# Paired activation halves in split fp32 products, with transposed modulation sums and a turned router product

## The chip, the cores and the metric

The kernel runs on one core of a Trainium2 chip. TensorE (PE) does the matrix products, VectorE (DVE), ScalarE (ACT) and GpSimd (POOL) the element-wise work, and sixteen DMA engines move data between HBM and SBUF. The metric is device time of one execution in microseconds (us); lower is better. Three runs of the kernel before took 2549.2, 2550.33 and 2555.16 us.

## The reference, cut to what matters

Everything is fp32. A first network of two layers works on 256 latent tokens and 256 context tokens of width 1024; a second block works on the 256 latent tokens alone. The parts that the change touches:

```python
# first network, layer l; cond is silu(c) for the latents, silu(c_ctx) for the context
m = cond @ w_ada[l] + b_ada[l]                       # (1024) @ (1024, 6144): the modulation
sh1, sc1, gt1, sh2, sc2, gt2 = split(m, 6)
xn = rms_norm(h, g_norm_mix[l]) * (1 + sc1) + sh1    # 512 tokens in all
p  = xn @ w_in[l]                                    # q, k, v, gates, ... of three branches
h  = h + gt1 * (sum_i sigmoid(gate_i) * (y_i @ w_branch[l, i])) @ w_out[l]
x2 = rms_norm(h, g_norm_ffn[l]) * (1 + sc2) + sh2
logits = x2 @ w_group, x2 @ w_router                 # 4 + 32 columns: the router
h  = h + gt2 * moe(x2)                               # top 2 of 32 experts
# in layer 1 the context gives only k and v, so queries and gates are 256 tokens
# second block, 256 tokens
z = rmsnorm(x, pre_mix_g) @ w_in_2                   # scan, short convolution, dilated attention
x = x + rmsnorm((sum_i sigmoid(h @ w_gate_i + b_i) * (y_i @ w_branch_2[i])) @ w_mix_out_2, post_mix_g)
gt = causal_dwconv(h @ w_ff_gate, ff_conv_w) + ff_conv_b
x = x + rmsnorm((gelu(gt) * (h @ w_ff_up)) @ w_ff_down, post_ffn_g)      # width 2816
```

## The kernel before, in words

**Split products.** PE's fast format (fp32r) drops low bits. So each factor of a dense product is split into a high part and a low rest, and three products are summed in one PSUM accumulator: high by high, high by low, low by high. A weight piece of 128 x 1024 values is copied by ACT to the high part `wh` (line 148), and DVE subtracts that from the raw weights to give `wl` (line 149). Each piece is split just before its use, with three buffers of `wh` and `wl` (four in the FFN), so DVE's and ACT's pace can hold PE.

**Two forms of dense product.** `dense_x` keeps activations stationary and streams 512 weight columns (lines 222 to 224); tokens end on partitions. `dense_w` keeps weights stationary and streams the tokens (lines 240 to 242); features end on partitions. The change is in `dense_w`: for one block of 128 output features (a column, below) and each 128 of the input it issues three products over n tokens. In layer 0 n is 512; in layer 1 and block 2 it is 256, and a product streams 256 columns. When a column's last product is done, its evacuation reads the accumulator: a gate's tanh on ACT, `G * acc` on DVE (line 454), in the FFN a scaled copy on ACT and two convolution steps on DVE (line 1623). Four accumulators of one PSUM bank each (512 fp32 values a partition) rotate.

**Modulation.** For the 24 pieces of 512 outputs (12 a layer) `ada_tile` multiplies with groups of array columns, which leaves partial sums on four groups of partitions; ACT copies them to `part`, and a product with the selection matrix `sel` adds them up. For the first eight pieces (shift and scale of the mixing) four small products give columns; for the other sixteen a single product of 512 columns in two passes gives a row (line 372). DVE adds a bias row that SP's queue has loaded, and POOL's queue writes the row to HBM scratch, from where it is read back broadcast. These pieces run as background between the products of the first layer's mixing; the queue of PE is in program order, and the order of instructions on each engine is set by the scheduler of the framework.

**Router.** For 256 tokens and each half of the features, `xr` (normalised tokens, features on partitions) is stationary and 36 columns of router weights stream: 16 passes (line 837). DVE scales the sums by the inverse root of the token's mean square.

The stretches, in us of the span: layer 0's mixing to some 640, its experts to 1130, layer 1's mixing 1240 to 1500, its experts to 1990, block 2's mixing to 2350 (scan, short convolution and gates 2036 to 2102, dilated attention to 2224, two more gated branches to 2317), FFN with gate and up 2352 to 2483, its last product to the end.

Of the kernel before, what the change touches and what calls it, by code (L numbers as in the profile page):

```python
# [8 lines left out]
FT = mybir.dt.float32  # L9
# [79 lines left out]

class Builder:  # L90
# [44 lines left out]
    def T(self, out, in_):  # L135
        k = in_.shape[0]
        self.nc.tensor.transpose(out, in_, self.ident[:k, :k])  # L137
# [55 lines left out]
    def dense_x(self, src, J, W, xh, xl, tts, evac, hold=0):  # L193

        if self.begun:
            ps, pieces, piece = self.begun.pop()
        else:
            self.tick()
            ps, pieces, piece = self.begin_x(src, J, W, xh, xl)
# [12 lines left out]
    def begin_x(self, src, J, W, xh, xl):  # L212
# [128 lines left out]
    def ada_tile(self, l, n, raw=None):  # L341
# [14 lines left out]
        if q < 2:  # L356
            for b in range(4):
                m = mm(ps[:, 2 * b:2 * b + 2], lhsT=part[:, b * 128:(b + 1) * 128], rhs=self.sel,
                       start=True, stop=True)
            if l == 0 and n in (0, 2):  # L360
                self.keep_warm(m, 6 if n else 3)
            for w in range(2):
                bias = self.vA[:, l * 48 + n * 4:l * 48 + n * 4 + 4]
                nc.vector.tensor_tensor(self.ada[l][:, q * 2 + w, half * 4:half * 4 + 4], ps[:, w:8:2], bias,
                                        op=OP.add)
            if q == 1:
                for w in range(2):
                    a = self.ada[l][:, 2 + w, half * 4:half * 4 + 4]
                    g = self.vA[:, 96 + l * 8 + half * 4:96 + l * 8 + half * 4 + 4]
                    nc.vector.scalar_tensor_tensor(a, a, 1.0, g, op0=OP.add, op1=OP.mult)  # L370
        else:
# [6 lines left out]
            if q == 4:  # L378
                gt = self.p_part.tile([2, 512], FT, name="grow", tag="row", bufs=2)
                nc.sync.dma_start(gt, bcast(I["g_norm_ffn"][l, half * 512:(half + 1) * 512], 2))  # L380
                nc.vector.scalar_tensor_tensor(row, row, 1.0, gt, op0=OP.add, op1=OP.mult)
            nc.gpsimd.dma_start(self.d_rows[l, q - 2, :, half * 512:(half + 1) * 512], row)
# [13 lines left out]
    def mix_norm(self, tp, l, h, mid=None, junk=None):  # L396

        nc = self.nc
        xh = self.p_x.tile([128, 8, 512], FR, name="xh", tag="xh")
        xl = self.p_x.tile([128, 8, 512], FR, name="xl", tag="xl")  # L400
# [11 lines left out]
        for k, (w, j) in enumerate(order):  # L412
            ws = slice(w * 256, w * 256 + 256)
            if k == 4 and mid is not None:
                mid(xh, xl)
# [8 lines left out]
            nc.vector.tensor_copy(xh[:, j:j + 2, ws], x)  # L424
            nc.vector.tensor_tensor(xl[:, j:j + 2, ws], x, xh[:, j:j + 2, ws].bitcast(FT), op=OP.subtract)
        return xh, xl

    def to_yT(self, y, n):

        yh = self.p_y.tile([128, 4, n], FR, name="yh", tag="yh")  # L430
        yl = self.p_y.tile([128, 4, n], FR, name="yl", tag="yl")
        for c in range(4):
# [3 lines left out]
            self.hilo(yh[:, c, :n], yl[:, c, :n], ps[:, :n])  # L436
        return yh, yl

    def gate_branch(self, i, gate_src, br_src, xh, xl, yh, yl, n, merged, bias=None):
        nc = self.nc  # L440
        for half in range(2):
# [15 lines left out]
            self.dense_w(gate_src[:, half * 512:(half + 1) * 512], 8, 512, xh, xl, n, ev_gate)  # L457
            self.dense_w(br_src[:, half * 512:(half + 1) * 512], 4, 512, yh, yl, n, ev_br)
# [31 lines left out]
    def mix(self, l, xh, xl):  # L490
# [19 lines left out]
        with self.tp("sg", 1, side="right") as sg:  # L510
# [15 lines left out]
            self.dense_x(W(O_ZB), 8, 512, xh, xl, tts, lambda t, ps: gelu2(u2[:, t], ps), hold=2)  # L526
# [14 lines left out]
            self.dense_x(W(O_ZB + 512), 8, 512, xh, xl, tts, ev_v)  # L541
            self.dense_x(W(O_VA), 8, 512, xh, xl, allt, lambda t, ps: nc.scalar.activation(v[:, t], ps, AF.Copy))
# [1268 lines left out]
```

## Time and profile before

| | |
|---|---|
| runs (us) | 2549.2, 2550.33, 2555.16; median 2550.33 |
| profiled execution | 2552.59 us, span 2550.6 us |
| granted TensorE clock | 0.983 mean |
| PE busy | 2431.7 us, 95% |
| DVE, ACT, POOL busy | 1334.0 us (52%), 857.1 us (34%), 134.6 us (5%) |
| DMA | 652.48 MB, 256 GB/s mean |

The profile is one execution. The profiled execution is 2.0 us longer than its span, and 2.3 us longer than the median. Busy shares are averages over stages with different limits, so a stretch is read by itself: a PE that is full there beside engines with room is the bound; where the DMA share is near 1, the transfers are. An engine's mean duration is a little longer than its pace, as successive instructions of one engine overlap; the pace is the distance of two starts in the timeline.

### The profile page before, as it was taken

To read this page: it belongs to the slowest core of one execution; us is meant where nothing else is said; L and a number is where in the kernel's file an instruction comes from. 1 tells how busy PE (TensorE), PEld (TensorE's weight loads), DVE (VectorE), ACT (ScalarE), POOL (GpSimd) and SP (SyncE) were. 2 spreads that over 40 slices of the span, in tenths; PEclk is the share of its full clock that TensorE was granted. 3 is DMA by queue.
4 is the path that set the end of the run, shared out by engine and by line. 5 is a ranking of instruction groups with operands and counts; after the bars stand their busy time and mean duration, and the time that the engine had idled before them with its cause. 6 is when DMAs were issued, how large, how long until landed. Compare 5 with 4: busy or idle time off the path is not lost. (4 is left out here: it accounts for less than half of the span.)

```text
span 2550.6 us, 33738 instructions
## 1 busy us (share of the span) xinstructions
PE 2431.7 (95%) x13632; PEld 1667.2 (65%) x13632; DVE 1334.0 (52%) x2767; ACT 857.1 (34%) x1510; POOL 134.6 (5%) x172
## 2 busy tenths in 40 slices
PE   8999999999899999989999879998988999999998
PEld 5766776678445554437888754443333898898997
DVE  4646535537444444457664553332223686656784
ACT  4334334434211111115444531111111544544663
POOL 1200002003100000001001110000000000000000
PEclk9999999999899999999999989999999999999999
DMA  9743544454899999983233669999999336435452
GB/s 327 219 162 117 174 145 142 147 184 148 345 422 420 421 421 420 421 355 134 99 124 113 193 270 422 421 421 421 421 421 405 134 132 207 149 116 206 156 175 99
DMA packets 177364, 652.48 MB, mean 256 GB/s; under 512 B 15174, under 2 KB 18778, under 8 KB 127666
## 3 DMA queue, kind: packets, MB, share of 16 engines
q1 hardware_dynamic: 169682, 626.97, 63.7%
q0 software_dynamic: 7520, 23.29, 3.1%
q8 instruction: 109, 1.79, 0.3%
q14 instruction: 53, 0.43, 0.0%
HBM read 644.42 MB, written 5.80 MB: 255 GB/s over the span
## 5 line engine op out<-in xcount | busy, mean ns | idle before, releaser
L149 DVE TENSOR_TENSOR wl<-raw,wh 128x1024 fp32r<-128x1024 f32 (+1 forms) x288 | 347.0, 1208 | 294.4 <-ACT wh L148 282.7
L963 PE MATMUL acc<-raw,xg 128*64 128x512 f32 x896 | 400.5, 597 | 25.1 <-DMA raw<-in_moe_w_up 13.3
L148 ACT ACTIVATE wh<-raw 128x1024 fp32r<-128x1024 f32 (+1 forms) x288 | 300.0, 1046 | 314.6 <-PE acc L241 159.0
L965 PE MATMUL acc<-raw,xg 128*64 128x512 f32 x896 | 400.8, 597 | 0.0
L240 PE MATMUL acc<-xh,wh 128*128 128x256 f32 (+1 forms) x1184 | 370.7, 314 | 0.5 <-ACT xh L157 0.5
L241 PE MATMUL acc<-xl,wh 128*128 128x256 f32 (+1 forms) x1184 | 371.0, 314 | 0.0
L242 PE MATMUL acc<-xh,wl 128*128 128x256 f32 (+1 forms) x1184 | 368.9, 312 | 0.1
L963 PEld LDWEIGHTS acc<-raw,xg 128*64 128x64 f32 x896 | 119.5, 137 | 279.1 <-issue 247.9
L240 PEld LDWEIGHTS acc<-xh,wh 128*128 128x128 f32 x1184 | 226.9, 192 | 19.9 <-issue 6.2
L241 PEld LDWEIGHTS acc<-xl,wh 128*128 128x128 f32 x1184 | 227.5, 192 | 14.0 <-issue 4.2
L242 PEld LDWEIGHTS acc<-xh,wl 128*128 128x128 f32 x1184 | 226.8, 192 | 13.9 <-issue 3.4
L222 PE MATMUL acc<-wh,xh 128*128 128x512 f32 x544 | 214.6, 395 | 2.2 <-ACT row L374 2.0
L224 PE MATMUL acc<-wh,xl 128*128 128x512 f32 x544 | 214.3, 395 | 0.0
L223 PE MATMUL acc<-wl,xh 128*128 128x512 f32 x544 | 213.8, 393 | 0.3 <-DVE wl L149 0.3
L987 PE MATMUL acc<-raw,hT 128*64 128x512 f32 x472 | 210.0, 596 | 1.5 <-ACT hT L979 1.5
L989 PE MATMUL acc<-raw,hT 128*64 128x512 f32 x472 | 210.0, 596 | 0.0
L993 DVE TENSOR_TENSOR aux<-aux,g 128x512 f32<-128x512 f32 x126 | 81.9, 694 | 199.1 <-PE aux L1074 199.1
L1099 DVE SCALAR_TENSOR_TENSOR yl<-acc,ws,yh 128x512 fp32r<-128x512 f32 x64 | 48.0, 750 | 221.3 <-ACT yh L1098 221.3
L987 PEld LDWEIGHTS acc<-raw,hT 128*64 128x64 f32 x472 | 61.8, 137 | 121.2 <-issue 114.7
L979 ACT ACTIVATE hT<-aux 128x512 f32<-128x512 f32 x32 | 19.1, 598 | 343.0 <-PE aux L137 343.0
L222 PEld LDWEIGHTS acc<-wh,xh 128*128 128x128 f32 x544 | 102.7, 189 | 29.8 <-issue 5.5
L965 PEld LDWEIGHTS acc<-raw,xg 128*64 128x64 f32 x896 | 119.5, 137 | 0.0
(482 smaller groups left out, 4248.2 us busy)
## 6 DMA issues: line engine op xcount, KB each, us to landing
raw<-in_moe_w_gate SPq DMA_DIRECT2D x59, 2048.0 KB
raw<-in_moe_w_down SPq DMA_DIRECT2D x59, 2048.0 KB
raw<-in_moe_w_up SPq DMA_DIRECT2D x53, 2048.0 KB
raw<-in_w_in SPq DMA_DIRECT2D x42, 2048.0 KB
raw<-in_w_ada SPq DMA_DIRECT2D x22, 2048.0 KB
rawx<-in_moe_w_up SPq DMA_DIRECT2D x11, 2048.0 KB
raw<-in_w_branch SPq DMA_DIRECT2D x18, 1024.0 KB
raw<-in_w_gate SPq DMA_DIRECT2D x6, 2048.0 KB
```

The source lines that it names most:

```text
L148: self.nc.scalar.activation(hi, src, AF.Copy)
L149: self.nc.vector.tensor_tensor(lo, src, hi.bitcast(FT), op=OP.subtract)
L222: mm(ps[t][:, :W], lhsT=a, rhs=wh[:, jj, :W], start=j == 0, stop=False)
L223: mm(ps[t][:, :W], lhsT=a, rhs=wl[:, jj, :W], start=False, stop=False)
L224: self.last_mm = mm(ps[t][:, :W], lhsT=b, rhs=wh[:, jj, :W], start=False, stop=j == J - 1)
L240: mm(ps[c][:, :n], lhsT=a, rhs=xh[:, j, :n], start=j == 0, stop=False)
L241: mm(ps[c][:, :n], lhsT=a, rhs=xl[:, j, :n], start=False, stop=False)
L242: mm(ps[c][:, :n], lhsT=b, rhs=xh[:, j, :n], start=False, stop=j == J - 1)
L963: mm(ps[0:64], lhsT=xg[:, j, a0:a0 + 64], rhs=wa(j), start=j == 0, stop=j == 7)
L965: mm(ps[64:128], lhsT=xg[:, j, b0:b0 + 64], rhs=wb(j), start=j == 0, stop=j == 7)
L987: mm(py[half][0:64], lhsT=hT[:, c, 0:64], rhs=da(c, half), start=c == 0, stop=c == 3)
L989: mm(py[half][64:128], lhsT=hT[:, c, 64:128], rhs=db(c, half), start=c == 0, stop=c == 3)
```

## The change

Three edits. First, where a stage has 256 tokens, the high and low parts of the activations lie side by side in one tile, (feature block, part, token). `dense_w` then streams both with one product of 512 columns against `wh`, and a second one of 256 columns adds `wl` by the high part. The accumulator then holds two sums of 256 tokens, and `by_both_sum` adds them with a DVE reduction into an SBUF tile that the evacuation reads. Stages of 512 tokens keep their form, except that the product for keys of branch C in layer 1 (512 tokens as two blocks of 256) becomes six products of 256 columns instead of three of 512. Second, `ada_tile` sums the partial sums by transposing them and reducing on DVE; for the sixteen row pieces the result is transposed back, and the biases and gains are taken as columns, without the row loads. Third, in the router the weights (padded to 64 columns, two groups of array columns) are stationary and the 256 tokens stream; a product with `fold` adds the two groups.

```diff
+    def by_both(self, ps, wh, wl, x, j, n, first, last):
+
         mm = self.nc.tensor.matmul
+        if x.paired and n == x.w:
+            mm(ps, lhsT=wh, rhs=x.blocks[0][:, j].rearrange("p k t -> p (k t)"), start=first, stop=False)
+            mm(ps[:, :n], lhsT=wl, rhs=x.hi(j, 0, n), start=False, stop=last)
+            return
+        for i in range(0, n, x.w):
+            k = min(x.w, n - i)
+            for w, part, at in ((wh, x.hi, 0), (wh, x.lo, 1), (wl, x.hi, 2)):
+                mm(ps[:, i:i + k], lhsT=w, rhs=part(j, i, i + k), start=first and i == at == 0,
+                   stop=last and at == 2 and i + k == n)
+
+    def by_both_sum(self, ps, x, n):
+        if not (x.paired and n == x.w):
+            return ps
+        s = self.p_whl.tile([128, 256], FT, name="sum", tag="sum", bufs=3)[:ps.shape[0]]
+        self.nc.vector.tensor_reduce(s, ps.rearrange("p (k t) -> p t k", k=2), axis=AX.X, op=OP.add)
+        return s
...
-                mm(ps[c][:, :n], lhsT=a, rhs=xh[:, j, :n], start=j == 0, stop=False)
-                mm(ps[c][:, :n], lhsT=a, rhs=xl[:, j, :n], start=False, stop=False)
-                mm(ps[c][:, :n], lhsT=b, rhs=xh[:, j, :n], start=False, stop=j == J - 1)
+                self.by_both(ps[c], a, b, x, j, n, j == 0, j == J - 1)
...
-            evac(c, ps[c])
+            evac(c, self.by_both_sum(ps[c], x, n))
...
+        for b in range(4):
+            m = self.T(ps[:, b * 128:(b + 1) * 128], part[:, b * 128:(b + 1) * 128])
+        if l == 0 and n in (0, 2):
+            self.keep_warm(m, 6 if n else 3)
+        rows = self.small(8, "rows").rearrange("p (w b) -> p w b", w=2)
+        nc.vector.tensor_reduce(rows, ps.rearrange("p (b g r) -> p r b g", b=4, g=4)[:, 0:2], axis=AX.X, op=OP.add)
...
+        nc.vector.tensor_tensor(a, rows, each(l * 48 + n * 4), op=OP.add)
...
+        if q > 1:
+            self.T(ps[0:8, 0:128], rows.rearrange("p w b -> p (w b)"))
+            row = self.p_part.tile([8, 128], FT, name="row", tag="row", bufs=2)
+            nc.scalar.activation(row, ps[0:8, 0:128], AF.Copy)
             for w in range(2):
...
-            mm(ps[0:2], lhsT=self.sel, rhs=part, start=True, stop=True)
-            row = self.p_part.tile([2, 512], FT, name="row", tag="row", bufs=2)
-            nc.scalar.activation(row, ps[0:2], AF.Copy)
-            bt = self.p_part.tile([2, 512], FT, name="brow", tag="row", bufs=2)
-            nc.sync.dma_start(bt, bcast(I["b_ada"][l, n * 512:(n + 1) * 512], 2))
-            nc.vector.tensor_tensor(row, row, bt, op=OP.add)
...
+            for c in range(4):
+                u = c % 2 * 64
+                mm(pl[u:u + 64, 0:256], lhsT=wrs[w][:, half * 4 + c], rhs=xr[:, c].rearrange("p k t -> p (k t)"),
+                   start=c < 2, stop=c >= 2)
...
             for k in range(2):
-                for c in range(4):
-                    mm(pl[:, k * 36:k * 36 + 36], lhsT=xr[k][:, c], rhs=wrs[w][:, half * 4 + c], start=c == 0, stop=c == 3)
...
+                mm(pl[:, 256 + k * 36:256 + k * 36 + 36], lhsT=lg[:, k * 128:(k + 1) * 128], rhs=fold[:, 0:36],
+                   start=True, stop=True)
```

The queue of PE in the FFN's gate product, before: three products for each of the input's blocks, `xh` and `xl` the activations, `wh` and `wl` the weights, one accumulator a column.

```order
L240 MATMUL acc_18886<-xh_17963,wh_18932 128x256
L241 MATMUL acc_18886<-xl_17964,wh_18932 128x256
L242 MATMUL acc_18886<-xh_17963,wl_18933 128x256
L240 MATMUL acc_18893<-xh_17963,wh_18928 128x256
L241 MATMUL acc_18893<-xl_17964,wh_18928 128x256
L242 MATMUL acc_18893<-xh_17963,wl_18929 128x256
```

The same place after, with `xb` the tile of both parts.

```order
L252 MATMUL acc_18379<-xb_17600,wh_18360 128x512
L253 MATMUL acc_18379<-xb_17600,wl_18361 128x256
L252 MATMUL acc_18364<-xb_17600,wh_18384 128x512
L252 MATMUL acc_18369<-xb_17600,wh_18384 128x512
L252 MATMUL acc_18374<-xb_17600,wh_18384 128x512
L252 MATMUL acc_18379<-xb_17600,wh_18384 128x512
L253 MATMUL acc_18364<-xb_17600,wl_18385 128x256
```

A triple has become a pair, and at the start of a piece the scheduler may bring the products with `wh` ahead of those with `wl`.

The queue of DVE where the gates of one FFN block are evacuated, before: `fa`, `fs` and `ga` are steps of convolution and GELU, `wl` the weight splits for later products.

```order
L149 TENSOR_TENSOR wl_18485<-raw_18450,wh_18484 128x1024
L1623 SCALAR_TENSOR_TENSOR fa_18378<-acc_18302,vB_380,fa_18378 128x255
L1623 SCALAR_TENSOR_TENSOR fa_18378<-acc_18302,vB_380,fa_18378 128x254
L1623 SCALAR_TENSOR_TENSOR fa_18399<-acc_18309,vB_380,fa_18399 128x255
L1625 SCALAR_TENSOR_TENSOR fs_18379<-fs_18379,fa_18378 128x256
L1623 SCALAR_TENSOR_TENSOR fa_18399<-acc_18309,vB_380,fa_18399 128x254
```

And after, with the sums in front of the steps that read them.

```order
L169 TENSOR_TENSOR wl_18017<-raw_18014,wh_18016 128x1024
L265 TENSOR_REDUCE sum_17946<-acc_17890 128x256
L169 TENSOR_TENSOR wl_18041<-raw_18014,wh_18040 128x1024
L1660 SCALAR_TENSOR_TENSOR fa_17948<-sum_17946,vB_382,fa_17948 128x255
L265 TENSOR_REDUCE sum_17965<-acc_17895 128x256
L1660 SCALAR_TENSOR_TENSOR fa_17948<-sum_17946,vB_382,fa_17948 128x254
```

Each column has one more DVE instruction, and it stands in the same queue as the splits that PE's next products need.

The queue of PE at a modulation piece in layer 0, before: L372 is the sum by the selection matrix, `glob` holds the constant matrices.

```order
L242 MATMUL acc_2276<-xh_198,wl_2273 128x512
L137 MATMUL aux_1764<-glob_89,P_1754 128x128 x2
L372 MATMUL acc_2250<-part_2261,glob_89 2x512
L629 MATMUL aux_1741<-vv_454,wT_1767 128x128
L581 MATMUL aux_1771<-kh_1056,qh_1054 128x256
```

And after, at a piece of the same kind.

```order
L157 MATMUL acc_2283<-glob_89,part_2294 128x128 x4
L258 MATMUL acc_2328<-xh_199,wh_2310 128x512
L157 MATMUL aux_1789<-glob_89,P_1779 128x128 x2
L258 MATMUL acc_2328<-xl_200,wh_2310 128x512
L157 MATMUL acc_2283<-glob_89,rows_2300 8x128
L258 MATMUL acc_2328<-xh_199,wl_2311 128x512
```

One product has become four transposes, and a fifth (of `rows`) that stands two products and two transposes further on and waits for DVE.

## Rows read from the trace of the kernel before

**Rows 1.** The page: busy time, chain that ended last, one group.

```profile
PE 2431.7 (95%) x13632; PEld 1667.2 (65%) x13632; DVE 1334.0 (52%) x2767; ACT 857.1 (34%) x1510; POOL 134.6 (5%) x172
...
PE 29%; DMA 9%; DVE 1%; ACT 0%; issue 0%; DVEq 0%; ACTq 0%
...
L148 ACT ACTIVATE wh<-raw 128x1024 fp32r<-128x1024 f32 (+1 forms) x288 | 300.0, 1046 | 314.6 <-PE acc L241 159.0
```

**Rows 2.** Stretches: busy us (count) PE, PEld, DVE, ACT, POOL; clock, DMA share, GB/s.

```profile
1430.00:1469.00 39.00, 32.38 (x248) 28.89 (x248) 22.96 (x56) 19.32 (x42) 4.50 (x7) 0.91 0.71 240
1600.00:1650.00 50.00, 49.89 (x250) 21.28 (x248) 17.22 (x34) 7.54 (x12) 0.00 (x0) 1.00 1.01 421
2036.00:2060.00 24.00, 22.83 (x200) 21.03 (x199) 22.34 (x49) 6.79 (x21) 0.53 (x1) 1.00 0.09 24
2060.00:2102.60 42.60, 42.59 (x355) 42.30 (x354) 31.98 (x71) 19.84 (x32) 0.00 (x0) 1.00 0.50 170
2281.00:2317.00 36.00, 35.92 (x297) 35.47 (x296) 22.76 (x37) 18.60 (x30) 0.00 (x0) 1.00 0.59 205
2352.50:2482.60 130.10, 130.10 (x1065) 129.82 (x1065) 101.09 (x182) 79.73 (x140) 0.00 (x0) 0.98 0.48 167
```

**Rows 3.** PE's timeline in the FFN: start us, duration, operation.

```profile
2449.83 0.28 PE L240 MATMUL acc<-xh,wh 128*128 128x256 f32 x1
...
2451.15 0.28 PE L242 MATMUL acc<-xh,wl 128*128 128x256 f32 x1
```

**Rows 4.** PE's timeline in layer 1's projection, products of 512 columns.

```profile
1488.86 0.40 PE L747 MATMUL acc<-wh,xl 128*128 128x512 f32 x1
...
1494.99 0.39 PE L747 MATMUL acc<-wh,xl 128*128 128x512 f32 x1
```

**Rows 5.** DVE's groups by shape: a reduction (busy us, mean ns).

```profile
L613 DVE TENSOR_REDUCE dax<-aux 128x1 f32<-128x512 f32 x32 | 20.6, 685 | 13.7 <-PE aux L581 13.7
```

**Rows 6.** DVE's timeline in the FFN.

```profile
2414.27 1.23 DVE L149 TENSOR_TENSOR wl<-raw,wh 128x1024 fp32r<-128x1024 f32 x1
2415.41 0.42 DVE L1627 SCALAR_TENSOR_TENSOR ga<-fs,fa 128x256 f32<-128x256 f32 x1
2415.75 0.42 DVE L1625 SCALAR_TENSOR_TENSOR fs<-fs,fa 128x256 f32<-128x256 f32 x1
2416.08 0.48 DVE L1623 SCALAR_TENSOR_TENSOR fa<-acc,vB,fa 128x255 f32<-128x255 f32 x1
2416.47 1.22 DVE L149 TENSOR_TENSOR wl<-raw,wh 128x1024 fp32r<-128x1024 f32 x1
```

**Rows 7.** DVE's groups by shape, FFN stretch.

```profile
L149 DVE TENSOR_TENSOR wl<-raw,wh 128x1024 fp32r<-128x1024 f32 x36 | 44.0, 1222 | 18.5 <-ACT wh L148 18.4
```

**Rows 8.** DVE's timeline behind layer 1's router.

```profile
1505.91 0.16 DVE L918 TENSOR_TENSOR gx<-L,m8g 128x8 f32<-128x8 f32 x1
...
1509.42 1.98 DVE L855 TENSOR_TENSOR x2l<-x,x2h 128x1024 fp32r<-128x1024 f32 x1
```

**Rows 9.** ACT's groups by shape: a copy that reads by steps.

```profile
L853 ACT ACTIVATE x2h<-x 128x1024 fp32r<-128x1024 f32 x6 | 12.6, 2131 | 9.1 <-DVE x L851 9.1
```

**Rows 10.** PE's timeline, attention of branch C in layer 1.

```profile
1433.10 1.09 PE L137 MATMUL aux<-glob,PC 128*128 128x128 f32 x4 [3.73 <-ACT PC L685]
```

**Rows 11.** PE's timeline at a modulation piece.

```profile
569.74 0.40 PE L241 MATMUL acc<-yl,wh 128*128 128x512 f32 x1
570.07 1.02 PE L372 MATMUL acc<-part,glob 128*2 128x512 f32 x2
571.02 0.50 PE L242 MATMUL acc<-yh,wl 128*128 128x512 f32 x1
```

**Rows 12.** PE's timeline, four transposes among products of 512 columns.

```profile
1483.59 0.60 PE L137 MATMUL aux<-glob,hm 128*128 128x128 f32 x4
1483.95 0.48 PE L749 MATMUL acc<-wh,xl 128*128 128x512 f32 x1
```

**Rows 13.** PE's timeline at layer 1's router.

```profile
1497.90 1.93 PE L837 MATMUL aux<-wr,xr 128*128 128x36 f32 x16
```

More of the change, by code (lines that the diff above doesn't have):

```diff
@@ L87, in bcast, with __init__, part, hi @@
     return bass.AP(tensor=ap.tensor, offset=ap.offset, ap=[[0, n]] + [list(x) for x in ap.ap])
+class Parts:
+    def __init__(self, w, *blocks):
+        self.w, self.blocks = w, blocks
+        self.paired = not isinstance(blocks[0], tuple)
+    def part(self, k, j, a, b):
+        i = a // self.w
+        x = self.blocks[i]
+        a, b = a - i * self.w, b - i * self.w
+        return x[:, j, k, a:b] if self.paired else x[k][:, j, a:b]
+    def hi(self, j, a, b):
+        return self.part(0, j, a, b)
+    def lo(self, j, a, b):
+        return self.part(1, j, a, b)
 class Builder:
@@ L136, in T @@
         k = in_.shape[0]
-        self.nc.tensor.transpose(out, in_, self.ident[:k, :k])
+        return self.nc.tensor.transpose(out, in_, self.ident[:k, :k])
     def keep_warm(self, after, n):
@@ new lines, in ada_tile @@
+        for b in range(4):
[4 more added lines that the diff above has]
+        nc.vector.tensor_reduce(rows, ps.rearrange("p (b g r) -> p r b g", b=4, g=4)[:, 0:2], axis=AX.X, op=OP.add)
+        each = lambda c: self.vA[:, None, c:c + 4].to_broadcast([128, 2, 4])
+        a = rows if q > 1 else self.ada[l][:, q * 2:q * 2 + 2, half * 4:half * 4 + 4]
@@ new lines, in ada_tile @@
+        nc.vector.tensor_tensor(a, rows, each(l * 48 + n * 4), op=OP.add)
+        if q in (1, 4):
+            nc.vector.scalar_tensor_tensor(a, a, 1.0, each((96 if q == 1 else 112) + l * 8 + half * 4), op0=OP.add,
+                                           op1=OP.mult)
+        if q > 1:
+            self.T(ps[0:8, 0:128], rows.rearrange("p w b -> p (w b)"))
+            row = self.p_part.tile([8, 128], FT, name="row", tag="row", bufs=2)
+            nc.scalar.activation(row, ps[0:8, 0:128], AF.Copy)
+            for w in range(2):
+                nc.gpsimd.dma_start(self.d_rows[l, q - 2, w, half * 512:(half + 1) * 512].rearrange("(b f) -> b f", f=128),
+                                    row[w * 4:w * 4 + 4])
@@ L398, in mix_norm @@
         nc = self.nc
-        xh = self.p_x.tile([128, 8, 512], FR, name="xh", tag="xh")
-        xl = self.p_x.tile([128, 8, 512], FR, name="xl", tag="xl")
+        if l == 0:
+            X = Parts(512, tuple(self.p_x.tile([128, 8, 512], FR, name=f"x{k}", tag=f"x{k}") for k in "hl"))
+        else:
+            X = Parts(256, *(self.p_x.tile([128, 8, 2, 256], FR, name=f"x{w}", tag=f"x{k}") for w, k in enumerate("hl")))
         a = self.ada[l]
@@ L423, in mix_norm @@
                                      bias=a[:, w, j + k:j + k + 1], scale=a[:, 2 + w, j + k:j + k + 1])
-            nc.vector.tensor_copy(xh[:, j:j + 2, ws], x)
-            nc.vector.tensor_tensor(xl[:, j:j + 2, ws], x, xh[:, j:j + 2, ws].bitcast(FT), op=OP.subtract)
-        return xh, xl
+            js = slice(j, j + 2)
+            hi, lo = (X.part(k, js, w * 256, w * 256 + 256) for k in range(2))
+            nc.vector.tensor_copy(hi, x)
+            nc.vector.tensor_tensor(lo, x, hi.bitcast(FT), op=OP.subtract)
+        return X
     def to_yT(self, y, n):
-        yh = self.p_y.tile([128, 4, n], FR, name="yh", tag="yh")
-        yl = self.p_y.tile([128, 4, n], FR, name="yl", tag="yl")
+        Y = self.parts_y(n)
         for c in range(4):
@@ L435, in to_yT, with parts_y, gate_branch @@
                 self.T(ps[:, t * 128:(t + 1) * 128], y[:, t, c * 128:(c + 1) * 128])
-            self.hilo(yh[:, c, :n], yl[:, c, :n], ps[:, :n])
-        return yh, yl
-    def gate_branch(self, i, gate_src, br_src, xh, xl, yh, yl, n, merged, bias=None):
+            self.hilo(Y.hi(c, 0, n), Y.lo(c, 0, n), ps[:, :n])
+        return Y
+    def parts_y(self, n):
+        if n == 256:
+            return Parts(256, self.p_y.tile([128, 4, 2, 256], FR, name="yb", tag="yb"))
+        return Parts(n, tuple(self.p_y.tile([128, 4, n], FR, name=f"y{k}", tag=f"y{k}") for k in "hl"))
+    def gate_branch(self, i, gate_src, br_src, x, y, n, merged, bias=None):
         nc = self.nc
@@ L488, in sg_weights, with mix @@
         return ws, hb
-    def mix(self, l, xh, xl):
+    def mix(self, l, X):
         nc, I, tc = self.nc, self.I, self.tc
@@ L804, in tail @@
             lgb.append(x)
+        fold = rp.tile([128, 64], FT, name="fold")
+        nc.vector.tensor_tensor(fold, self.ident[:, 0:64], self.ident[:, 64:128], op=OP.add)
         L = rp.tile([128, nt, 40], FT, name="L")
@@ L813, in moe_in @@
                 part["sb"], part["ab"] = self.row_bc(rp, l, 1, w, "sb"), self.row_bc(rp, l, 2, w, "ab")
-                part["lg"], part["ss"] = rp.tile([128, 2, 36], FT, name="lg"), self.small(4, "ss")
+                part["lg"], part["ss"] = rp.tile([128, 256], FT, name="lg"), self.small(4, "ss")
                 part["x"] = [rp.tile([128, D], FT, name="x2", tag="x2", bufs=2) for _ in range(2)]
```

170 lines of the change are left out of this document (71 added, 99 removed).

## Prediction

> **What bounds the kernel now.** I read the busy line and the chain of waits first. TensorE (PE) is busy for 2431.7 of 2550.6 us, and PE leads the chain before DMA and far before the vector engine, DVE [rows 1]. PE's work is therefore the thing to shorten, but "busy" is an average, so I then read the stretches [rows 2]. In the expert phases, as 1600 to 1650, the transfers fill the time (DMA share 1.01, 421 GB/s); the change leaves those alone. In layer 1 and block 2 the share is 0.09 to 0.71 and PE is full, except at 1430 to 1469, where it works 32.38 of 39 us. The column to look at beside PE is DVE's: 101.09 of 130.1 us in the FFN, 31.98 of 42.6 at 2060, 22.34 of 24 at 2036, 22.76 of 36 at 2281. The change moves work from PE to DVE in just these stretches.
>
> **PE's side of the pairing.** A 256-column product starts every 0.120 us: 11 steps from 2449.83 to 2451.15 [rows 3]. A 512-column one starts every 0.227 us: 27 steps from 1488.86 to 1494.99 [rows 4]. At the upper clock level, 2.4 GHz, which the FFN and the stretch at 2060 are granted almost throughout (0.98 and 1.00 in [rows 2]), 256 columns are 0.107 us and 512 are 0.213, so both widths pay about 0.013 us a product above their columns. Three products of 256 cost 0.360 us; one of 512 and one of 256 cost 0.347. The change saves one of those 0.013 per triple and no columns. There are 1088 triples with 256 tokens: 320 in layer 1, 416 in block 2's mix, 352 in the FFN; that is -4.2, -5.4 and -4.6 us, -14.2 in all, if nothing else happens. The KC product of layer 1, which had 512 columns, now runs as two blocks of 256: 32 x (6 x 0.120 - 3 x 0.227) = +1.2 us.
>
> **The price of the sum.** Every one of the 161 columns now ends in a DVE reduction that reads 512 PSUM values, taking two values 1 KB apart for each output, and every evacuation waits for it. No such read is in the trace, so I bound it. The nearest operation is the reduction of 512 PSUM values side by side, 685 ns [rows 5]; such DVE operations overlap by about 0.08 us (the 1.23 us split is followed after 1.14 [rows 6]), so 0.61 us. The nearest access pattern is a read by steps of 32 bytes, from SBUF: a subtraction over 1024 values takes 1.98 us so, against 1.222 us for the split side by side [rows 7, 8], and ScalarE (ACT) takes 2131 ns for a stepped copy against 1046 [rows 1, 9]. Half of DVE's 1.98 is 0.99 us for 512. A value below 0.61 is excluded, since each operation passes 512 values at the rate of the plain row. Between 0.61 and 0.99 I take 0.99: the ACT row has one stepped input like the reduction, and it doubled. The Trainium skill, page "SBUF — State Buffer", section "Door 1: The DMA port swizzle (why `[64,N]` ≈ `[32,N]`)", says SBUF is read in lines of 16 bytes and PSUM in lines of 8, with a penalty for each step to a new line; rows 8 and 9 agree for SBUF, no row shows it for PSUM, and by it the sum is the one below. Another page of the Trainium skill, "VectorE: DVE Perf Modes", section "Mode 1× (REGULAR) — the baseline", says of the plain one-value-per-cycle mode that fp32, "weird strides" and PSUM operands all work; by that the price would be 0.61 and the result that of rival 1.
>
> **FFN (2352.5 to 2482.6).** A cycle of four gate and four up columns has on DVE eight splits of 1.14 us, eight convolution steps of 0.39 (2416.08 to 2416.47) and sixteen other operations of 0.34 (2415.41 to 2415.75) [rows 6, 7]: 17.7 us. PE has 64 triples in it, 23.0 us before and 22.2 after. With eight reductions DVE has 22.6 at 0.61, level with PE, or 25.6 at 0.99, above it. There are 5.5 cycles: 140.8 us at 0.99 against 130.1 now. Four split pieces can stand ahead when the stretch begins, 4.6 us of cover, so I take +6 (up to +11). At 0.61, PE keeps the lead: -4.
>
> **Block 2's mix.** At 2036 to 2060 the scan's DVE chain takes 22.34 of 24 us in 49 operations [rows 2], and the eight reductions of the first two convolution products queue in it: 22.34 + 7.9 = 30.3, or 26.3 with the overlaps (49 x 0.08) taken off; +2.3 to +6.3, I take +4. At 2060 to 2102.6 twenty reductions make 31.98 + 19.8 = 51.8 us in 42.6, or 46.1 without the overlaps of 71 operations: +3.5 to +9.2, I take +5. At 2281 to 2317 sixteen make 38.6 or 35.6 in 36 us: +0.5. Elsewhere (2224 to 2281, the first product) DVE has room and PE's saving counts: -2. Sum +7.5. At 0.61 the same sums give +1 at 2036, -0.2 at 2060, -1.2 at 2281 (PE's own saving) and -2 elsewhere: -2.4.
>
> **Layer 1.** DVE works 22.96 of 39 us at 1430 [rows 2], so throughput is no limit. But twenty of the 52 reductions stand in the attention of branch C, whose DVE steps PE waits for: at 1433.10 it idles 3.73 us for PC [rows 10]. If all are hidden the layer gains 4.2 - 1.2 = 3.0; if all twenty are seen it loses 19.8 - 3.0 = 16.8. I take a third seen, as only part of the chain waits on DVE: +4.
>
> **Modulation.** For sixteen tiles the two passes of the row sum go: 570.07 to 571.02 holds PE 1.05 us (1.28 from 569.74 to 571.02, less one 0.23 product) [rows 11]. Four transposes replace them, 0.36 us (1483.59 to 1483.95), and one back, a quarter of that, 0.09 [rows 12]. That saves 0.60 x 16 = 9.6. But the transpose back needs a reduction and an addition on DVE, 0.16 us each for such small ones (1505.91, 0.16) [rows 8], behind at worst a split of 1.14: 1.46 us, while PE has two 512-column products and two transposes between, 0.64 (as the order of layer 0 shows). A stall is thus between 0 and 0.8; I take 0.35: 16 x 0.35 = 5.6, net -4 (-9.6 to +3). PE runs in order, so everything behind a stalled transpose waits too. The two row writes instead of one go out on POOL's queue long before anyone reads them, and the sixteen bias loads that leave SP's queue were hidden. ACT gets one short row copy a tile as before and, by the order, loads its function table seven times instead of five; at 34% busy [rows 1] that is free. The eight tiles that summed by pairs of columns get four transposes instead of four small products: 0.
>
> **Router.** Sixteen passes of 36 columns take 1.93 us on the way to the top-2 choice [rows 13]. Now eight passes of 256 columns in two halves of the array: 8 x 0.12 = 0.96 or less. Only the last block of each of two layers stands on the path; the extra sum and fold lie beside the root that scales them, so -1.5 (-4 to 0).
>
> **Sum.** 6 + 7.5 + 4 - 4 - 1.5 = +12 on the profiled execution's 2552.6 (span 2550.6 and 2.0 around it), so 2564.6. That execution lies 2.3 above the median, 2550.3: **2562 us**.
>
> **Rival 1: the sum is cheap.** The reduction costs 0.61 us: the plain row speaks for it, ACT's and DVE's stepped rows against. FFN -4, mix -2.4, layer 1 at a third of 20 x 0.61 less 3.0: +1, modulation and router -5.5: -10.9, and 2539 us, not slower. Between the two prices the total crosses zero at 0.61 + 0.38 x 10.9/22.9 = 0.79 us a reduction; above that the kernel is slower. It would span 2531 to 2552.
>
> **Rival 2: the turn through DVE.** Cheap reductions, but DVE has a split and a 512-value operation in front of each modulation tile's reduction, and PE has nothing between: a stall of 1.14 + 0.61 + 0.32 = 2.07 us a tile, and 16 x 2.07 - 9.6 = +23.5 in place of -4 makes 2567, slower. From 1.5 us a tile it decides (2543 + 16 x 1.5 - 9.6 = 2557). For it: PE takes its work in order, and DVE works 52% of the span [rows 1]. Against it: the 0.64 us of PE work between.
>
> **Rival 3: the long product hides its fixed part.** If the pair costs its columns alone, 0.320 us, 736 triples outside the FFN save 29 and the FFN, held by DVE at 124 us, 6; with +1.2 for KC, +7 of waits and -5.5: 2518 us. Rows 4 speak against it: neighbours of 512 columns show the same 0.013.
>
> **How the numbers follow.** Chances: forecast 0.52 (its own range 2550 to 2574), rival 1 0.37, rival 2 0.07, rival 3 0.04. About 0.3% (7.7 us) is what this measurement can tell from no change, so faster means under 2542.7 and slower over 2558.0. Forecast: 0.03 faster, 0.11 same, 0.38 slower; rival 1: 0.23, 0.13, 0.01; rival 2: 0, 0.03, 0.04; rival 3: 0.04. Sum 0.30, 0.27, 0.43. The range runs from rival 1's lower part, 2534, to 2578, where FFN, mix and layer 1 stand near their upper bounds.
>
> **What would show it.** The mean of the reduction's row: near 1.07 us for the forecast, near 0.69 for rival 1. In the FFN, DVE near full and PE waiting for splits, in a stretch of about 136 us; under rival 1 PE stays full in 126. A 512 product followed by a 256 one must start 0.347 us before the next pair. In layer 0, PE's wait in front of the transpose back tells rival 2. I am wrong if reductions cost under 0.79 us, or if DVE stays below PE in the FFN and 2060 stretches at 0.99.

## The result and the profile after

The changed kernel takes 2575.06 us (median of 2572.62, 2574.27, 2575.84 and 2578.32) against 2550.51 before: ratio 1.0094, 95% interval 1.0079 to 1.0108. It is 24.5 us slower; I had forecast 11.7 (2562). The sign came out as forecast, the loss is twice the forecast one, and the mechanism that I gave the most chance was not the one.

The profiled execution took 2572.62 us, its span is 2570.8. First the page's busy line and the chain that ended last, as in [rows 1]:

```profile
PE 2429.7 (95%) x12612; PEld 1617.6 (63%) x12612; DVE 1417.0 (55%) x2945; ACT 854.9 (33%) x1512; POOL 141.1 (5%) x188
...
PE 26%; DMA 9%; DVE 4%; ACT 1%; issue 1%; DVEq 0%; ACTq 0%
```

PE is busy for 2 us less, in a span that is 20 longer; DVE is busy for 83 us more, and has 4% of the chain where it had 1%. The row that decides between my price and rival 1's is the reduction's, from DVE's groups by shape (the last figure of the first part is the mean in ns); its pace is in DVE's timeline, where two of them start 1.20 us before the next operation:

```profile
L265 DVE TENSOR_REDUCE sum<-acc 128x256 f32<-128x512 f32 x160 | 108.0, 686 | 17.9 <-PE acc L253 17.0
```

```profile
2329.80 1.28 DVE L265 TENSOR_REDUCE sum<-acc 128x256 f32<-128x512 f32 x2
2331.00 0.75 DVE L491 SCALAR_TENSOR_TENSOR G<-G,sum 128x256 f32<-128x256 f32 x2
```

686 ns, 0.60 us each: the plain reduction's 685 in [rows 5], not the 0.99 of the stepped reads in [rows 8, 9]. The pair of products is as forecast too. PE's timeline in the FFN; seven pairs take 2.42 us, 0.346 each:

```profile
2451.40 0.39 PE L252 MATMUL acc<-xb,wh 128*128 128x512 f32 x1
2451.63 0.28 PE L253 MATMUL acc<-xb,wl 128*128 128x256 f32 x1
...
2453.82 0.40 PE L252 MATMUL acc<-xb,wh 128*128 128x512 f32 x1
```

So the two prices of rival 1, the sum's and the pair's, hold, and yet the kernel is slower. To see where, I matched the instructions that both kernels have in equal number (same source line, same count) and subtracted their starts. The table gives the median shift against the kernel before, in us, around some points of its span; it is worked out from one trace of each kernel, and the columns to the right are the experiments below (E9's up to 664 only).

| us of before | changed | E1 no sums | E2 no pairs | E3 old modulation | E4 plain convolution | E9 later transpose |
|---|---|---|---|---|---|---|
| 62 | -0.4 | -0.5 | -0.6 | -0.2 | -0.8 | 0.0 |
| 147 | +5.7 | +6.7 | +5.8 | -1.5 | +5.2 | -2.7 |
| 582 | +4.9 | +3.9 | +6.9 | +0.1 | +5.2 | +8.3 |
| 664 | +8.2 | +7.0 | +11.8 | +3.2 | +8.1 | +10.6 |
| 1238 | +7.6 | +6.4 | +11.7 | +2.8 | +7.4 | |
| 2033 | +7.7 | +9.5 | +12.0 | +2.7 | +7.9 | |
| 2060 | +10.3 | +12.1 | +12.0 | +5.3 | +7.9 | |
| 2131 | +18.4 | +11.4 | +12.0 | +13.5 | +7.7 | |
| 2350 | +22.1 | +9.8 | +11.9 | +17.0 | +11.4 | |
| 2482 | +20.4 | +6.5 | +12.0 | +15.5 | +10.4 | |

Three places carry it: the start of layer 0 (+6), block 2's scan and short convolution (+11 between 2033 and 2131), the gates to 2350 (+4). Layer 1 costs nothing and the FFN gains 1.7. Another +3.3 comes between 582 and 664.

An early row is good to some 4 us. In the profiles of E7 and E8 PE, DVE, ACT and POOL run the instructions of before in the same order for the first 1200 us, and yet their shift at 147 is -2.2 and -3.8, and grows by 1.5 and 1.6 from 582 to 664. So about half of the +3.3 is the one execution of before that was profiled. The start of layer 0 stands clear of this: the five profiles with the new modulation as it is (the changed kernel, E1, E2, E4, E5) have +5.2 to +6.8 at 147, the six others with the old one (E3, E7, E8, E10, E11, E12) -4.2 to -1.5.

Block 2 first. PE's waits from 2036 to 2112 (waited for; us in total, times, longest); before, 2030 to 2105 had only 1.0 us of waits, for gK:

```profile
PE acc L253 <- DVE wl L169: 5.3, 2, 2.7
PE aux L1481 <- DVE gK L1474: 0.9, 2, 0.6
PE acc L252 <- DVE sum L265: 0.8, 1, 0.8
```

The product waits not for the reduction but for a weight split, twice for 2.67 us. What the second split stood behind is in DVE's timeline (`su` and `sy` are steps of the short convolution):

```profile
2084.83 0.69 DVE L265 TENSOR_REDUCE sum<-acc 128x256 f32<-128x512 f32 x1
2085.43 0.47 DVE L1527 SCALAR_TENSOR_TENSOR sy<-su,vC,sy 128x254 f32<-128x254 f32 x1
2085.82 0.42 DVE L1523 TENSOR_TENSOR su<-su,sum 128x256 f32<-128x256 f32 x1
2086.15 0.68 DVE L265 TENSOR_REDUCE sum<-acc 128x256 f32<-128x512 f32 x1
...
2088.79 1.22 DVE L169 TENSOR_TENSOR wl<-raw,wh 128x1024 fp32r<-128x1024 f32 x1
```

And what PE does after it, in its own timeline:

```profile
2090.07 0.58 PE L253 MATMUL acc<-xb,wl 128*128 128x256 f32 x1 [2.67 <-DVE wl L169]
2090.45 0.63 PE L252 MATMUL acc<-xb,wh 128*128 128x512 f32 x1
...
2093.65 0.63 PE L252 MATMUL acc<-xb,wh 128*128 128x512 f32 x1
2094.08 0.42 PE L253 MATMUL acc<-xb,wl 128*128 128x256 f32 x1
2094.29 0.63 PE L252 MATMUL acc<-xb,wh 128*128 128x512 f32 x1
```

A pair takes 0.64 us here (2093.65 to 2094.29) instead of 0.346: the lower of the two clock levels. The stretches say so (the figure before the last two is the granted clock):

```profile
2060.00:2065.00 5.00, 3.06 (x10) 2.33 (x12) 5.00 (x7) 0.63 (x1) 0.00 (x0) 0.58 0.00 0
2065.00:2070.00 5.00, 5.00 (x36) 4.73 (x36) 1.15 (x7) 2.07 (x13) 0.54 (x1) 0.74 0.90 313
2085.00:2090.00 5.00, 1.56 (x8) 0.75 (x6) 5.00 (x12) 0.60 (x1) 0.00 (x0) 0.81 0.00 0
2090.00:2095.00 5.00, 4.93 (x17) 4.36 (x18) 2.92 (x5) 1.06 (x1) 0.00 (x0) 0.50 0.00 0
```

The first two lines are the first of the two waits, the last two the second. In both, DVE is full (5.00 of 5) while PE idles, and PE pays again afterwards. Before, the clock at 2036 to 2102 was 1.00 throughout [rows 2]. From 2090.07 to 2094.7 PE does in 4.6 us what takes some 2.5 at the upper level, so a wait of 2.67 us costs about 4.8 (worked out from these rows).

No sum stands in front of the first split. It starts at 2060.67, and DVE's first sum of the stretch at 2070.59:

```profile
2060.67 1.21 DVE L169 TENSOR_TENSOR wl<-raw,wh 128x1024 fp32r<-128x1024 f32 x1
...
2070.59 0.68 DVE L265 TENSOR_REDUCE sum<-acc 128x256 f32<-128x512 f32 x1
```

Between the split before it and this one DVE has 44 operations, most of them steps of the scan; in the kernel before, in E2 and in E4 there are 38, and PE does not wait for that split. In E1, with pairs and without sums, there are 44 again. So the first wait came with the pairs, by the order that the scheduler made for them, and only the second with the sums.

The +4 to 2350 is a third wait of this kind, and the longest: 4.62 us, for the first splits of the output product (`w_mix_out_2`), which are behind the sums and merging steps of the last gated branch.

```profile
2337.83 0.79 PE L243 MATMUL acc<-wl,xb 128*128 128x512 f32 x1 [4.62 <-DVE wl L169]
```

```profile
2332.34 1.29 DVE L265 TENSOR_REDUCE sum<-acc 128x256 f32<-128x512 f32 x2
2333.53 0.76 DVE L491 SCALAR_TENSOR_TENSOR G<-G,sum 128x256 f32<-128x256 f32 x2
2334.20 0.76 DVE L492 TENSOR_TENSOR merged<-merged,G 128x256 f32<-128x256 f32 x2
2334.87 1.77 DVE L178 SCALAR_TENSOR_TENSOR xb<-merged,xb 128x256 fp32r<-128x256 f32 x5
2336.54 3.50 DVE L169 TENSOR_TENSOR wl<-raw,wh 128x1024 fp32r<-128x1024 f32 x3
```

Neither the kernel before nor E2 waits there, and E1 waits 0.7 us.

At the start of layer 0 the chain is of the same kind with other names. PE's waits from 60 to 140, then DVE's timeline behind the longest:

```profile
PE acc L157 <- DVE rows L402: 3.1, 1, 3.1
PE aux L157 <- DVE yb L588: 2.7, 2, 2.2
PE acc L157 <- ACT part L391: 0.9, 1, 0.9
```

```profile
93.88 0.18 DVE L399 TENSOR_REDUCE rows<-acc 128x8 f32<-128x32 f32 x1
93.99 1.25 DVE L191 SCALAR_TENSOR_TENSOR rst<-rsy,rsh 128x1 f32<-128x1 f32 x1
95.17 0.68 DVE L561 SCALAR_TENSOR_TENSOR vn<-gs,vn 128x512 f32<-128x512 f32 x1
95.77 1.21 DVE L195 SCALAR_TENSOR_TENSOR rsy<-rst,rsy 128x1 f32<-128x1 f32 x1
96.91 0.15 DVE L402 TENSOR_TENSOR rows<-rows,vA 128x8 f32<-128x8 f32 x1
```

The reduction of `rows` and the addition to it are 0.18 and 0.15 us long, but three steps of a layer norm stand between them, and the transpose back waits for both. Two of the three work on one value a partition and yet take 1.25 and 1.21 us. Each ends some 15 ns after an operation of POOL ends, by the trace at 95.23 and 96.97; POOL's timeline has the first of these, and two merged in its second line:

```profile
93.97 1.26 POOL L575 TENSOR_TENSOR vn<-vn,lg 128x512 f32<-128x512 f32 x1 [1.35 <-DVE rsy L195]
95.19 3.02 POOL L576 TENSOR_TENSOR vn<-vn,lb 128x512 f32<-128x512 f32 x2
```

The clock after it is 0.82 and 0.84:

```profile
95.00:100.00 5.00, 2.88 (x9) 2.14 (x10) 5.00 (x12) 0.27 (x1) 3.73 (x4) 0.82 0.05 7
100.00:105.00 5.00, 5.00 (x20) 4.01 (x20) 4.78 (x10) 1.06 (x1) 3.08 (x3) 0.84 0.00 0
```

### The profile page after: what moved, and what is told of

The parts are those of the page before. It is cut to its first block, busy times and chain, and to the rows that moved or that the text cites. A ratio compares the mean times of both kernels' runs of the same rounds, so it can differ in the third digit from the quotient of the medians.

```text
span 2570.8 us, 31817 instructions
## 1 busy us (share of the span) xinstructions
PE 2429.7 (95%) x12612; PEld 1617.6 (63%) x12612; DVE 1417.0 (55%) x2945; ACT 854.9 (33%) x1512; POOL 141.1 (5%) x188
## 5 line engine op out<-in xcount | busy, mean ns | idle before, releaser
L252 PE MATMUL acc<-xb,wh 128*128 128x512 f32 x672 | 239.7, 403 | 1.0 <-DVE sum L265 0.8
L253 PE MATMUL acc<-xb,wl 128*128 128x256 f32 x672 | 187.7, 288 | 6.2 <-DVE wl L169 6.1
L252 PEld LDWEIGHTS acc<-xb,wh 128*128 128x128 f32 x672 | 127.8, 192 | 28.3 <-DVE sum L265 1.3
L253 PEld LDWEIGHTS acc<-xb,wl 128*128 128x128 f32 x672 | 129.8, 193 | 12.1 <-DVE wl L169 9.9
L265 DVE TENSOR_REDUCE sum<-acc 128x256 f32<-128x512 f32 x161 | 108.7, 686 | 17.9 <-PE acc L253 17.0
L1140 ACT ACTIVATE yh<-acc,ws 128x512 fp32r<-128x512 f32 x64 | 44.0, 687 | 208.0 <-PE acc L1031 208.0
L258 PE MATMUL acc<-xh,wh 128*128 128x512 f32 x256 | 103.1, 403 | 0.0
L258 PE MATMUL acc<-xh,wl 128*128 128x512 f32 x256 | 102.2, 399 | 0.0
L258 PE MATMUL acc<-xl,wh 128*128 128x512 f32 x256 | 101.8, 398 | 0.0
L1129 DVE SCALAR_TENSOR_TENSOR hid<-hid,acc 128x512 f32<-128x512 f32 x32 | 22.0, 688 | 141.4 <-PE acc L1007 141.4
```

Source lines behind the costliest of these rows:

```text
L252: mm(ps, lhsT=wh, rhs=x.blocks[0][:, j].rearrange("p k t -> p (k t)"), start=first, stop=False)
L253: mm(ps[:, :n], lhsT=wl, rhs=x.hi(j, 0, n), start=False, stop=last)
L258: mm(ps[:, i:i + k], lhsT=w, rhs=part(j, i, i + k), start=first and i == at == 0, stop=last and at == 2 and i + k == n)
L265: self.nc.vector.tensor_reduce(s, ps.rearrange("p (k t) -> p t k", k=2), axis=AX.X, op=OP.add)
```

## The experiments

The kernel before was timed beside each of the four sets, and its median lay between 2550.5 and 2552.0 us.

**E1, no sums.** What do the reductions cost, wherever they stand?

```diff
-        s = self.p_whl.tile([128, 256], FT, name="sum", tag="sum", bufs=3)[:ps.shape[0]]
-        self.nc.vector.tensor_reduce(s, ps.rearrange("p (k t) -> p t k", k=2), axis=AX.X, op=OP.add)
-        return s
+        return ps
```

> The changed kernel with the 161 reductions left out: evacuations read the first 256 values of the accumulator, so the low activations times the high weights are missing from the result. All products stay. Theory A (the reductions, though they cost only the plain price of 0.69 us, make the vector engine late in block 2's mix; PE then waits for weight splits and comes back at a lower clock): block 2's mix falls from 15 us over before to about 5 us under it, the FFN to 4 under, layer 1 to 3 under; what is left is the 5 us of the modulation at the start and the 3 of layer 0's router; about 2548 to 2552. Theory B (the pair of products itself is slow, or its accumulator is held too long): block 2's mix stays at least 8 us over before, total 2565 or more.

Measured: 2558.2 us, ratio 1.0028 (1.0018 to 1.0037). So the sums cost 16.9 of the 24.5 us, and theory B falls. But I expected 2548 to 2552: without sums block 2's mix should have gained, and from 2033 to 2350 it only stays level (+9.5 to +9.8). The first of the two waits for a split is still there (2.7 us), since DVE's order through the scan is that of the changed kernel; with the clock behind it, it takes back what the pair saves in this stretch.

**E2, no pairs.** The three products of 256 again, on the new tiles.

```diff
-        if x.paired and n == x.w:
+        if self.both_on and x.paired and n == x.w:
```

(`both_on` is false, in `by_both_sum` as well.)

> The changed kernel with three products of 256 columns again in place of the pair, no reductions; modulation, router and the tiles of the halves as in the change. Theory A: what is left is modulation (+5) and router (+3), and +1 for the product that lost its 512 columns: 2558 to 2560. Theory B agrees here. Theory C (the modulation and router cost nothing net, the +8 at the end of layer 0 is a shift of the order that comes with the rest): 2551.

Measured: 2559.9 us, 1.0034 (1.0021 to 1.0047), as theory A had it; theory C falls. The shift is made by 664 us and is flat from there, so the tiles and the product that lost its 512 columns cost nothing that can be seen. Against E1 the pair saves 1.7 us of the 14.2 that its products should save on PE; the intervals of the two runs overlap, so this cannot be told from nothing.

**E3, old modulation.**

```diff
-        for b in range(4):
-            m = self.T(ps[:, b * 128:(b + 1) * 128], part[:, b * 128:(b + 1) * 128])
...
+        else:
+            mm(ps[0:2], lhsT=self.sel, rhs=part, start=True, stop=True)
...
```

> The changed kernel with the modulation sums of before. Theory A: the +5.5 us at 121 us of the span goes (PE waited 3.1 us for the transpose back and ran at a clock of 0.83 to 0.92 after it), the rest stays: 2568 to 2571. Theory C: 2575.

Measured: 2566.5 us, 1.0053 (1.004 to 1.0066): 8.6 us back, somewhat more than expected, and the wait for `rows` is gone.

**E4, plain convolution.** Twelve of 161 columns unpaired (`both_on` starts true here and is asked as in E2):

```diff
+            self.both_on = False
             self.dense_w(W(2064), 8, 512, X, 256, lambda c, ps: nc.scalar.activation(u[:, c], ps[:, :256], AF.Copy))
             self.dense_w(W(2576), 8, 512, X, 256, ev_x)
             self.dense_w(W(1552), 8, 512, X, 256, ev_b)
+            self.both_on = True
```

> The changed kernel with the three products of the short convolution (12 of 161 columns) unpaired, in three products of 256 columns and without a reduction. Theory A: the two waits of 2.7 us for weight splits between 2054 and 2090 and the lower clock after them go, 9 to 11 us: 2564 to 2566. A rival, that every reduction costs the same wherever it stands (24.5/161 = 0.15 us each): 12 x 0.15, 2573.

Measured: 2563.7 us, 1.0047 (1.0034 to 1.006): 11.3 us for these twelve columns. PE's waits in the same stretch of it:

```profile
PE aux L1482 <- DVE gK L1475: 1.0, 2, 0.6
```

Both waits for splits are gone, and the rival of an equal cost for each reduction with them. The third, of 4.6 us before the output product, is still there.

**E12, both at once** (the diffs of E3 and E4 together).

> The changed kernel with the modulation of before and the short convolution's three products unpaired, both at once. If the two losses are separate places that add up (8.6 and 11.3 us when each was taken out alone): 2575.1 - 19.9 = 2555. Rival (either one only moves the other's wait): 2560 or more.

Measured: 2553.8 us, 1.0008 (0.9999 to 1.0017). They add up. With 149 of the 161 columns still paired and summed, the kernel cannot be told from before: what these two places cost is as much as the whole loss. That does not make the rest free. The third wait is in this run too (4.6 us), and E4 and E12 still lose 3.7 and 3.8 us from 2131 to 2350; savings elsewhere, as of the first gates after 2224 and of the FFN, make up for it.

**E5, old router.**

```diff
-            for c in range(4):
-                u = c % 2 * 64
-                mm(pl[u:u + 64, 0:256], lhsT=wrs[w][:, half * 4 + c], rhs=xr[:, c].rearrange("p k t -> p (k t)"),
-                   start=c < 2, stop=c >= 2)
...
+                for c in range(4):
+                    mm(pl[:, k * 36:k * 36 + 36], lhsT=xr[k][:, c], rhs=wrs[w][:, half * 4 + c], start=c == 0, stop=c == 3)
```

> The changed kernel with the router of before. Theory A: the 3 us that layer 0's end lost (offset of equal instructions from 4.9 at 582 us of the span to 8.2 at 664) go: 2571 to 2573. Rival (the loss there is a wait for other work, and the router is free): 2575.

Measured: 2579.9 us, 1.0113 (1.0098 to 1.0129), slower by 4.8, which the two intervals do not quite part: both theories missed. By the shifts of equal instructions it had lost 2.8 more than the changed kernel already at 582 us, ahead of the first router, 1.2 more at 664 and 5.4 more at 2033; so more than the router differs between these two runs, and this one does not price it.

**E10, the turned router alone,** on the kernel before (the diff of E5 the other way round).

> The kernel before with the turned router alone (no pairs, modulation of before). On the changed kernel the old router cost 4.8 us, though equal instructions show only 1 to 3 of them at the two routers. If the router itself is worth that: 2546. If its worth is the -1.5 that I forecast: 2549. If most of e5's loss was order elsewhere: 2550 to 2552.

Measured: 2551.2 us, 0.9999 (0.999 to 1.0008). The router in itself gives nothing that can be told. PE's wait for `M`, which is made from the top-2 choice, is 1.5 us shorter in each layer (5.3 for 6.8 and 10.7 for 12.2); in layer 1, 1.2 of this goes to two waits at the turned product, for `xr` and `lg`, that the old one did not have. Why the old one cost 4.8 us among the other edits stays open: the shifts show where, not why.

**E6, no transpose back.** The rows go to scratch by elements:

```diff
-            self.T(ps[0:8, 0:128], rows.rearrange("p w b -> p (w b)"))
-            row = self.p_part.tile([8, 128], FT, name="row", tag="row", bufs=2)
-            nc.scalar.activation(row, ps[0:8, 0:128], AF.Copy)
             for w in range(2):
-                nc.gpsimd.dma_start(self.d_rows[l, q - 2, w, half * 512:(half + 1) * 512].rearrange("(b f) -> b f", f=128),
-                                    row[w * 4:w * 4 + 4])
+                nc.gpsimd.dma_start(self.d_rows[l, q - 2, w, half * 512:(half + 1) * 512].rearrange("(b f) -> f b", f=128),
+                                    rows[:, w])
```

> The changed kernel without the transpose back of the sixteen modulation rows: POOL's queue writes the columns to scratch element by element, 1024 values a piece. Theory A (the PE queue stands behind the transpose back, which waits for vector operations: 3.06 us at 97 us, then a clock of 0.84): most of the 8.6 us that the old modulation gave back is given back here too, 2567 to 2570. Rival (the four transposes and the order cost it, not the wait): 2573 to 2576.

Measured: 2626.7 us, 1.0298 (1.0279 to 1.0316). The experiment put a larger cost in the place of the one it took out: the shift grows from +22 at 121 us to +61 at 568, while the pieces come. POOL's queue also loads the attention's bias, and waits 158.8 us in all ahead of those loads (128.1 before). It says nothing on the wait; it does say that those writes are not free.

**E9, transpose back later.** At the start of the next piece instead:

```diff
+        if self.rows_back:
+            self.rows_back.pop()()
         ps = self.acc() if raw is None else self.aux()
...
+            def back():
+                ps = self.aux()
+                self.T(ps[0:8, 0:128], rows.rearrange("p w b -> p (w b)"))
...
+            self.rows_back.append(back)
...
```

> The changed kernel with each modulation piece's transpose back (and its copy and writes) issued at the start of the next piece instead of right behind the reduction, so that PE does not wait for the vector engine there. Theory A (the wait of 3.06 us at 97 us and the lower clock behind it are what the modulation lost): that wait goes and 5 to 8 us with it, 2567 to 2570. Rival (the four transposes and the order cost it): 2574 to 2576.

Measured: 2578.1 us, 1.0098 (1.0082 to 1.0114), not faster. But at 147 us the shift is -2.7, as in the profiles with the old modulation, where the changed kernel has +5.7: the wait and what follows it cost some 8 us there, as theory A has it. Between 288 and 296 us it loses 16.6 at once. PE's waits of E9 from 230 to 290, and its stretch:

```profile
PE aux L158 <- DVE P L664: 5.6, 3, 2.7
PE aux L158 <- DVE rst L195: 3.2, 1, 3.2
PE aux L672 <- ACT wT L670: 1.9, 4, 0.5
```

```profile
230.00:280.00 50.00, 39.24 (x206) 27.00 (x205) 27.69 (x99) 18.07 (x64) 0.66 (x1) 0.82 0.07 23
```

The changed kernel's stretch, with the attention at about the same place:

```profile
235.00:285.00 50.00, 49.94 (x276) 33.92 (x275) 31.84 (x103) 22.62 (x69) 3.52 (x6) 1.00 0.27 86
```

The attention of layer 0, which had background products between its softmax steps (PE 49.94 of 50 us busy), has fewer of them there now (39.24, 206 products for 276). One place was mended and another lost its cover.

**E7, FFN alone,** on the kernel before, and **E8, the same with each reduction done twice.**

```diff
+        self.both_on = True
         self.blk_ffn(x, y, X, vB)
```

(Block 2 keeps the tiles of the halves, in E10 and E11 too.)

> The kernel before with the pair and its reduction in the FFN's gate and up products alone (44 of 161 columns). By the changed kernel's FFN, which ends 2.8 us nearer to before than it begins, 2.5 to 3.5 us under before: ratio 0.9988. Had a reduction cost 0.99 us as I forecast, 6 over before.

> The same with every reduction done twice (the second writes the same values). It tries the forecast's sum for the FFN at a price known by now: the vector engine then has 17.7 + 16 x 0.61 = 27.5 us a cycle against PE's 22.2, 151 us in 5.5 cycles, less 4.6 us of splits that stand ahead, against 130.1: 16 to 21 us over before. Rival (PE waits for the release of accumulators, which the reduction brings earlier, so a second one costs its own 0.61 us at the end of a block only): 44 x 0.61 / 4 = 7 us or less.

E7: 2549.4 us, 0.9998 (0.9989 to 1.0007), no change that can be told; the 2.5 to 3.5 us that I expected lie at and beyond the edge of that interval (-2.8), and the 6 over of a price of 0.99 outside it. E8: 2581.7 us, 1.0126 (1.011 to 1.0142), 31 over before; the sum gave 16 to 21. PE's waits from 2350 to 2512 in E8:

```profile
PE acc L253 <- DVE sum L267: 16.1, 19, 1.6
PE acc L254 <- DVE wl L170: 1.5, 3, 0.5
```

```profile
2350.00:2510.00 160.00, 141.17 (x720) 115.22 (x720) 147.78 (x266) 84.36 (x139) 0.00 (x0) 0.94 0.39 135
```

DVE works 147.78 of 160 us there, PE 141.17 at a clock of 0.94. The 44 second reductions are 26.8 us at 0.61 and cost 32 (2581.7 less 2549.4): they are paid in full and some 5 us more. PE waits for sums, that is for accumulators to be released, as the rival had it; the rival's 7 us is out, and my cover of 4.6 us is not seen.

**E11, router and FFN** (the edits of E10 and E7 together), as a candidate for a better kernel.

> The kernel before with the turned router and the pair in the FFN alone. The sum of its parts: 1.1 us (the FFN alone measured 2549.4 against 2550.5) and what the router alone shows: 2545 to 2550.

Measured: 2549.8 us, 0.9993 (0.9984 to 1.0002). No version found beats the kernel before by more than the measurement can tell.

## Why the prediction was right or wrong, point by point

- **PE's pace: right.** 0.346 us a pair against 0.347. What followed from it was not: without sums (E1) the 14.2 us on PE come to 1.7 against E2, which cannot be told from nothing. In E1's profile the FFN keeps 3.3 of its 4.6, and the wait for the scan's split with the clock after it takes some 4.8 back; what took the rest is not shown.
- **The price of the sum: wrong.** I took the stepped rows' 0.99 us and gave 0.37 to the plain row's 0.61; it is 0.60. In this kernel the step of 1 KB in PSUM adds nothing to a DVE reduction (686 against 685 ns). The rule on lines in the Trainium skill, "SBUF — State Buffer", section "Door 1: The DMA port swizzle (why `[64,N]` ≈ `[32,N]`)", agrees with rows 8 and 9 for SBUF and does not carry over to this read; what the page says there of PSUM's lines it says of matmuls. The sentence of the Trainium skill's page "VectorE: DVE Perf Modes", section "Mode 1× (REGULAR) — the baseline", that I quoted agrees with the 686 ns.
- **FFN: wrong by the price.** +6 forecast, -1.7 in the changed kernel's profile (the 130.1 us take 128.4), and nothing that can be told in E7's times; rival 1 had -4. E8 shows that the balance of DVE against PE decides there once DVE has more to do, and more harshly than I reckoned.
- **Block 2's mix: right place, wrong reason, half the size.** +7.5 forecast at 0.99, +14.4 measured at 0.60 (2033 to 2350). I summed DVE's work over a stretch and compared it with the stretch. With 0.61 that gave -2.4. The loss is in the order of the queue: three splits behind short steps of scan, convolution and merging, 2.67, 2.67 and 4.62 us of PE, and the lower clock after each. The first of them has no sum in front of it, so no price of the sum could have told it.
- **Layer 1: wrong.** +4 forecast, 0 measured (+7.6 at 1238, +7.7 at 2033). A third of twenty reductions seen was a guess; E1 without sums is no faster there. The 3.73 us in [rows 10], which I read as a wait for DVE, ended by ACT.
- **Modulation: the step that failed most.** -4 forecast; taking it out gives 8.6 back (E3). I bounded the stall at 0.8 us by a split of 1.14 in front; it was 3.1 once, behind a layer norm's chain of which two steps lasted until POOL was done, with the clock after it. That is rival 2's mechanism, at one piece rather than at sixteen, and I gave it 0.07. E9 confirms the place (some 8 us), though not a remedy. Nor were all the bias loads hidden, as I took them to be: in the profile of before PE idles 2.00 us at 131.39 for a row that waits for such a load (0.2 us in E7).
- **Router: not decided.** -1.5 forecast; alone its interval is -2.6 to +2.0 us (E10). The shorter way to the top-2 choice is there, and most of it is spent beside it in layer 1.
- **What no term held: the clock.** All my terms were durations at the upper level. Each new wait of 2.7 to 4.6 us was followed by PE at the lower one; after the second split's 2.67 us that is another 2.1.

So the sum was +12 by a price that was wrong, and it lacked two effects that were larger: the place of an instruction in its queue, and the clock. That the kernel is slower, as forecast, is luck: my own sign of being wrong, a reduction under 0.79 us, came true, and with the right price of sum and pair rival 1 said 2539, the other way.

## What to carry to other kernels

A saving on the busiest engine counts only where what it needs next is ready: here 14 us less PE work gave nothing that could be told (1.7), and part of it went into a wait for a split. When an edit adds short steps to an in-order queue, look for the instruction in that queue for which the full engine waits, and count what stands ahead of it at that place, not the stretch's average. Compare that order before and after even where no step was added, since the scheduler may move the instruction. Add the price of the clock to every new wait of PE.

## What the runs showed of the hardware that I had not expected

- A DVE reduction over pairs 1 KB apart in PSUM runs at the pace of one over neighbours: 686 against 685 ns.
- After PE had idled 2.67 us it ran a pair in 0.64 us instead of 0.346 from 2090.07 to about 2094.7, at a granted clock of 0.50.
- DVE operations on one or two values a partition can last until an operation of POOL ends. The two above took 1.25 and 1.21 us; the same line (L195) took 0.15 just before, at 93.81. In the traces of before, the changed kernel, E3 and E9 every DVE operation on 128 partitions and at most 32 values a partition that took over 0.5 us (eight in each trace) ended 12 to 29 ns after a POOL operation on two tensors; the longest, 2.36 us at 1514.68 of the changed kernel, ended with one at 1517.02. Others beside POOL were not held (L402 at 96.91, 0.15 us). What POOL and DVE share there, no run here shows.
